# Gate products in column pairs, half of the inner dimension as seven-product blocks, and the first input split on VectorE

## The chip, the core and the metric

The kernel runs on one core of one Trainium2 chip. The metric is the device time of one launch in microseconds (us). Before the change three runs took 2828.03 to 2828.67 us, median 2828.26 us.

## What is computed

Two layers of a post-norm encoder for 256 tokens of width 2048, all in float32. A layer reads its input x (256 x 2048) and computes, cut to what matters:

```
h  = x @ w_in                      # 2048 x 4608: queries, keys, values of three mixers
ya, yb, yc = three attentions      # 1024, 512 and 512 wide
ga, gb, gc = split(sigmoid(x @ w_gate + b_gate), 3)          # 2048 x 6144
mix = ga * (ya @ w_br_a) + gb * (yb @ w_br_b) + gc * (yc @ w_br_c)
x  = layer_norm(ALPHA * x + mix @ w_out)
g, u = split(x @ w_ffn_in, 2)                                # 2048 x 11264
x  = layer_norm(ALPHA * x + (silu(g) * u) @ w_ffn_out)       # 5632 x 2048
```

## The kernel before

**Float32 by three products.** Every operand is held as a high part in the matmul's own number type and a low part that is the rest. A product is three matmuls: high by high, high by low, low by high. `split_unit` (L69) makes the parts of a weight block of 256 x 512 (two k-steps of 128): ACT casts the high part (`wh`), DVE subtracts it (`wl`). There are 5 buffers for raw blocks (`raw`) and 6 for each of `wh` and `wl`, so the splits run at most 6 blocks ahead of TensorE. SP's queue issues the loads in order. The parts of x (`xh`, `xl`) are the stationary operands, 128 x 128, for the two token tiles t = 0, 1.

**The plain product.** `gemm` (L94) computes 512 columns: for each block two k-steps, two token tiles and three matmuls, 12 matmuls on 512 columns. Its accumulators are two of the four banks of `psA`. After each block `pump` lets one step of side work (`side`: head transposes, attention) into the program.

**Two columns together.** In the feed-forward part `pair_gemm` (L571) computes the gate column and the up column of one 512-wide chunk f together, in seven accumulator banks p1, p6, p7, p2, p3, q4, q5. Of the 16 k-steps, 0 to 3 go as a seven-product block (Strassen's scheme in Winograd's form, over two halves of k and the two token tiles), 4 and 5 as a smaller one of single k-steps, and the others (`four`, L606) as plain products that add into the same banks. In all 61 steps of three matmuls, 183 matmuls, where two plain columns take 192. The sums that the scheme needs: of x by `x_sums` (L530, once a layer, as side work), of the weight blocks on DVE inside `pair_gemm` (`u`, `hub`, `e`, L620 to L647). Eight operations at its end (L660 to L667) join the banks. The block `hub` lives in two buffers of its own, not in `raw`. Chunk f = 0 goes by two plain products, under which `x_sums` runs; chunks 1 to 10 go by `pair_gemm`.

**Feed-forward groups.** Chunks 0 to 2, 3 to 5, 6 to 8 and 9 to 10 form four groups. After each chunk two token tiles are multiplied out (L684 to L691), transposed on TensorE (`hidTp`, L692) and split (`rl`, L694). After each group four columns of w_ffn_out are multiplied (L700) and added to the residual.

**Gates.** Twelve plain columns of w_gate, four per branch (L425 to L449). Each is followed by its column of the branch's projection, of 4 or 2 blocks. After the very first one the remaining side work is drained (L435).

**Start.** `x_lhs` (L152) loads the two tiles of a 512-wide chunk of x, transposes them on TensorE, casts on ACT and subtracts on DVE.

**End.** The last column of the last group takes its last 8 k-steps token tile by token tile (`tail=8`, L701), so that the layer norm of tile 0 can begin under the matmuls of tile 1.

The order on each engine is made by the scheduler of the kernel's language from data dependences and the program's order; each engine then works through its list in order. The page numbers the lines of the whole file; the functions that the change touches:

Of the kernel before, what the change touches and what calls it, by code (L numbers as in the profile page):

```python
# [33 lines left out]
def trunk_kernel(ctx: ExitStack, tc: tile.TileContext, x, w_in, sinks, lq1, lk1, lq2, lk2, diff_g,  # L34
# [33 lines left out]

    def split_unit(raw):  # L69
        h = wpool.tile([P, UK, CW], F32R, tag="wh", name="wh", bufs=6)  # L70
        l = wpool.tile([P, UK, CW], F32R, tag="wl", name="wl", bufs=6)
        n = raw.shape[1]
# [21 lines left out]
    def gemm(src, kw0, nk, c0, lhs, tail=0):  # L94
# [5 lines left out]
        def mm3(t, kt, w, j):  # L100
            (wh, wl), (ah, al) = w, lhs(kt, t)
            nc.tensor.matmul(acc[t], ah, wh[:, j, :], start=kt == 0, stop=False)  # L102
            nc.tensor.matmul(acc[t], ah, wl[:, j, :], start=False, stop=False)  # L103
            nc.tensor.matmul(acc[t], al, wh[:, j, :], start=False, stop=kt == nk - 1)  # L104

        for k in range(0, nk - tail, UK):
            lhs(k, 0)
            w = load_unit(src, kw0 + k, c0)
            for j in range(UK):
                for t in range(NT):  # L110
                    mm3(t, k + j, w, j)
# [13 lines left out]

    def bcast(vec, c0, name):
        t = scr.tile([P, CW], F32, tag="bc", name=name, bufs=4)
        nc.gpsimd.dma_start(t, vec[c0:c0 + CW].partition_broadcast(P))
        return t
# [16 lines left out]
    def set_x(c, t, src):  # L146
# [3 lines left out]
        split(xh[c][t], xl[c][t], pv)  # L150

    def x_lhs(kt, t):  # L152
        c = kt // 4
        if xh[c][t] is None:
# [3 lines left out]
            for u in range(NT):  # L158
                set_x(c, u, x0[u])
# [15 lines left out]
    for layer in range(DEPTH):  # L175
# [48 lines left out]
        def v_heads(acc, col0, slots):  # L224
            for i, s in enumerate(slots):
                for t in range(NT):
                    nc.scalar.copy(s[:, t * P:(t + 1) * P], acc[t][:, col0 + i * P:col0 + (i + 1) * P])

# [122 lines left out]
        sink = const.tile([P, AQ], F32, tag="sink", name="sink")  # L351
        nc.sync.dma_start(sink, sinks[layer].partition_broadcast(P))
        nsink = const.tile([P, AQ], F32, tag="nsink", name="nsink")
        nc.vector.tensor_scalar_mul(nsink, sink, -1.0)

        lv = const.tile([P, 4, 64], F32, tag="lv", name="lv")
        for i, v in enumerate((lq1, lk1, lq2, lk2)):
            nc.sync.dma_start(lv[:, i, :], v[layer].partition_broadcast(P))
        lp = const.tile([P, 2, 64], F32, tag="lp", name="lp")
        nc.vector.tensor_mul(lp, lv[:, 0::2, :], lv[:, 1::2, :])  # L360
        ls = const.tile([P, 2], F32, tag="ls", name="ls")
        nc.vector.tensor_reduce(ls, lp, AX.X, ALU.add)
        le = const.tile([P, 2], F32, tag="le", name="le")
        nc.scalar.activation(le, ls, AF.Exp)
        lam = const.tile([P, 1], F32, tag="lam", name="lam")
        nc.vector.tensor_sub(lam, le[:, 0:1], le[:, 1:2])
        nc.vector.tensor_scalar_add(lam, lam, lam_init)

        gcol = const.tile([P, 1], F32, tag="gcol", name="gcol")
        nc.sync.dma_start(gcol, diff_g[layer].rearrange("(p o) -> p o", o=1))  # L370
        nc.vector.tensor_scalar_mul(gcol, gcol, 1.0 - lam_init)
# [3 lines left out]
        relb = const.tile([P, NHC, 3 * P], F32, tag="relb", name="relb")  # L375
        for h in range(NHC):
            raw = tmp("hank")[:, :SEQ]
            row = rel_bias[layer, h]
            nc.sync.dma_start(raw, bass.AP(row.tensor, row.offset + 129, [[1, P], [1, SEQ]]))
            nc.vector.tensor_add(relb[:, h, 0:P], raw[:, 0:P][:, ::-1], mask_b[:, 0:P])  # L380
            nc.vector.tensor_add(relb[:, h, P:3 * P], raw[:, ::-1], mask_b[:, P:3 * P])
# [37 lines left out]
        mixT = [None] * NCH  # L419
        for b, (wbr, nk, y0i) in enumerate(((w_br_a, 8, 0), (w_br_b, 4, 2), (w_br_c, 4, 3))):  # L420
# [4 lines left out]
            for c in range(NCH):  # L425
                bg = bcast(b_gate[layer], b * D + c * CW, "bg")
                acc = gemm(w_gate[layer], 0, 16, b * D + c * CW, x_lhs)
                gs = []
                for t in range(NT):
                    g = tmp("gate")  # L430
                    nc.vector.tensor_add(g, acc[t], bg)
                    nc.scalar.activation(g, g, AF.Sigmoid)
                    gs.append(g)
                if b == 0 and c == 0:
                    drain()  # L435
                acc = gemm(wbr[layer], 0, nk, c * CW, y_lhs)
                for t in range(NT):
                    if b == 0:
                        mix[c][t] = act.tile([P, CW], F32, tag=f"fb{c * NT + t}", name=f"mix{c}{t}")
                        nc.vector.tensor_mul(mix[c][t], gs[t], acc[t])  # L440
                    else:
                        nc.vector.tensor_mul(gs[t], gs[t], acc[t])
                        nc.vector.tensor_add(mix[c][t], mix[c][t], gs[t])
                if b == 2:
                    mixT[c] = ychunk(c)
                    for t in range(NT):
                        pv = transpose4(mix[c][t], "mixTp")
                        s = slice(t * P, (t + 1) * P)
                        split(mixT[c][0][:, :, s], mixT[c][1][:, :, s], pv)  # L449
# [66 lines left out]


        sums = {}
        turn = [0]

        def sum_tiles():
            pair = const.tile([P, 2, 4, P], F32R, tag="relb", name="sums")
            for i in range(6):
                yield act.tile([P, 4, P], F32R, tag=f"fa{i}", name="sums")
            for i in range(2):
                yield pair[:, i]
            while True:
                yield scr.tile([P, 4, P], F32R, tag="bc", name="sums", bufs=4)

        def x_sums(delay):  # L530


            yield from wait(delay)
            tiles = sum_tiles()
            for c in range(NCH):
                z = []
                for t in range(NT):
                    v = tmp("z").rearrange("p (k q) -> p k q", k=4)
                    nc.vector.tensor_add(v, xh[c][t].bitcast(F32), xl[c][t].bitcast(F32))
                    z.append(v)  # L540
                yield
                n = (2, 1, 0, 0)[c]
                if n:
                    a11, a12, a21, a22 = (v[:, j:j + n, :] for v in z for j in (0, n))
                    p = tmp("zs").rearrange("p (k q) -> p k q", k=4)
                    q = tmp("zs").rearrange("p (k q) -> p k q", k=4) if n == 2 else p[:, 2:4]
                    s1, s2, s3, s4 = p[:, 0:n], p[:, n:2 * n], q[:, 0:n], q[:, n:2 * n]
                    nc.vector.tensor_sub(s1, a21, a22)
                    nc.vector.tensor_sub(s3, a11, a21)
# [204 lines left out]
```

## Time and profile before

| | us |
|---|---|
| runs, median (lowest to highest) | 2828.26 (2828.03 to 2828.67) |
| the profiled execution, its own time | 2827.89 |
| its span, first to last instruction | 2826.0 |
| busy: TensorE matmul (PE) | 2791.0 |
| busy: VectorE (DVE) | 1966.3 |
| busy: ScalarE (ACT) | 1349.6 |

The span is what the trace resolves; about 1.9 us of the execution lie around it. PE is busy for 99% of the span, in every slice but the first and the last; matmuls overlap in the pipeline, so a matmul's own duration (390 ns) is longer than the distance from one to the next. That distance, with the number of matmuls, is what sets the time.

### The profile page before, as it was taken

To read this page: it belongs to the slowest core of one execution; us is meant where nothing else is said; L and a number is where in the kernel's file an instruction comes from. 1 tells how busy PE (TensorE), PEld (TensorE's weight loads), DVE (VectorE), ACT (ScalarE), POOL (GpSimd) and SP (SyncE) were. 2 spreads that over 40 slices of the span, in tenths; PEclk is the share of its full clock that TensorE was granted. 3 is DMA by queue.
4 is the path that set the end of the run, shared out by engine and by line. 5 is a ranking of instruction groups with operands and counts; after the bars stand their busy time and mean duration, and the time that the engine had idled before them with its cause. 6 is when DMAs were issued, how large, how long until landed. Compare 5 with 4: busy or idle time off the path is not lost. (4 is left out here: it accounts for less than half of the span.)

```text
span 2826.0 us, 33866 instructions
## 1 busy us (share of the span) xinstructions
PE 2791.0 (99%) x12660; PEld 2296.8 (81%) x12660; DVE 1966.3 (70%) x2282; ACT 1349.6 (48%) x1722; POOL 60.7 (2%) x110
## 2 busy tenths in 40 slices
PE   8999999999999999999999999999999999999998
PEld 6887888887888888888878888888878888888886
DVE  5656555566986877868776565555579779688686
ACT  4455444443554544545445454444435545455452
POOL 0000000000000000000000000000000000000000
PEclk9999999999999999999999999999999999999999
DMA  7555666665665666665764556666656656656564
GB/s 255 171 164 175 202 200 205 203 209 177 198 204 190 194 202 193 194 201 177 229 216 153 179 177 202 201 204 202 209 162 214 200 190 196 203 186 208 186 198 141
DMA packets 282660, 549.20 MB, mean 194 GB/s; under 512 B 19840, under 2 KB 21376, under 8 KB 282496
## 3 DMA queue, kind: packets, MB, share of 16 engines
q1 hardware_dynamic: 276096, 526.07, 58.1%
q0 software_dynamic: 6400, 20.98, 2.6%
q8 instruction: 99, 1.62, 0.2%
q14 instruction: 65, 0.53, 0.1%
HBM read 542.78 MB, written 4.19 MB: 194 GB/s over the span
## 5 line engine op out<-in xcount | busy, mean ns | idle before, releaser
L74 DVE TENSOR_TENSOR wl<-raw,wh 128x1024 fp32r<-128x1024 f32 x972 | 1182.6, 1223 | 718.0 <-ACT wh L73 713.6
L73 ACT CAST wh<-raw 128x1024 fp32r<-128x1024 f32 x972 | 1019.2, 1054 | 1239.1 <-PE acc L104 809.4
L102 PE MATMUL acc<-wh,xh 128*128 128x512 f32 x1472 | 582.2, 396 | 6.9 <-ACT xh L54 6.9
L103 PE MATMUL acc<-wl,xh 128*128 128x512 f32 x1472 | 575.8, 391 | 3.6 <-DVE wl L74 2.0
L104 PE MATMUL acc<-wh,xl 128*128 128x512 f32 x1472 | 576.2, 392 | 0.2 <-DVE xl L55 0.2
L103 PE MATMUL acc<-wl,rh 128*128 128x512 f32 x1216 | 474.3, 390 | 0.0
L102 PE MATMUL acc<-wh,rh 128*128 128x512 f32 x1216 | 473.8, 390 | 0.0
L104 PE MATMUL acc<-wh,rl 128*128 128x512 f32 x1216 | 473.7, 390 | 0.0
L102 PEld LDWEIGHTS acc<-wh,xh 128*128 128x128 f32 x1472 | 277.1, 188 | 66.2 <-ACT xh L54 9.1
L103 PEld LDWEIGHTS acc<-wl,xh 128*128 128x128 f32 x1472 | 277.3, 188 | 61.9 <-DVE wl L74 4.1
L104 PEld LDWEIGHTS acc<-wh,xl 128*128 128x128 f32 x1472 | 277.0, 188 | 59.6 <-DVE xl L55 2.2
L102 PEld LDWEIGHTS acc<-wh,rh 128*128 128x128 f32 x1216 | 228.3, 188 | 47.3
L103 PEld LDWEIGHTS acc<-wl,rh 128*128 128x128 f32 x1216 | 228.3, 188 | 47.2
L104 PEld LDWEIGHTS acc<-wh,rl 128*128 128x128 f32 x1216 | 228.3, 188 | 46.9
L595 PE MATMUL q<-wh,xl 128*128 128x512 f32 x460 | 179.2, 390 | 0.0
L591 PE MATMUL q<-wh,xh 128*128 128x512 f32 x460 | 179.1, 389 | 0.0
L593 PE MATMUL q<-wl,xh 128*128 128x512 f32 x460 | 179.0, 389 | 0.0
L595 PE MATMUL p<-wh,sums 128*128 128x512 f32 x380 | 149.0, 392 | 0.0
L591 PE MATMUL p<-wh,sums 128*128 128x512 f32 x380 | 148.9, 392 | 0.0
L593 PE MATMUL p<-wl,sums 128*128 128x512 f32 x380 | 147.8, 389 | 0.0
L74 DVE TENSOR_TENSOR wl<-u,wh 128x1024 fp32r<-128x1024 f32 (+1 forms) x100 | 111.4, 1114 | 37.2 <-ACT wh L73 37.2
L73 ACT CAST wh<-u 128x1024 fp32r<-128x1024 f32 (+1 forms) x100 | 96.7, 967 | 78.6 <-PE p L595 39.8
(184 smaller groups left out, 2509.1 us busy)
## 6 DMA issues: line engine op xcount, KB each, us to landing
raw<-in_w_ffn_in_dram SPq DMA_DIRECT2D x332, 512.0 KB, 3.6
raw<-in_w_gate_dram SPq DMA_DIRECT2D x192, 512.0 KB, 4.2
raw<-in_w_ffn_out_dram SPq DMA_DIRECT2D x176, 512.0 KB, 3.7
raw<-in_w_in_dram SPq DMA_DIRECT2D x144, 512.0 KB, 3.6
raw<-in_w_out_dram SPq DMA_DIRECT2D x64, 512.0 KB, 4.0
raw<-in_w_br_a_dram SPq DMA_DIRECT2D x32, 512.0 KB, 4.1
hub<-in_w_ffn_in_dram SPq DMA_DIRECT2D x20, 512.0 KB, 3.4
raw<-in_w_br_b_dram SPq DMA_DIRECT2D x16, 512.0 KB, 4.6
```

What stands on the lines that cost most here:

```text
L73: nc.scalar.copy(h[:, 0:n], raw)
L74: nc.vector.tensor_sub(l[:, 0:n], raw, h[:, 0:n].bitcast(F32))
L102: nc.tensor.matmul(acc[t], ah, wh[:, j, :], start=kt == 0, stop=False)
L103: nc.tensor.matmul(acc[t], ah, wl[:, j, :], start=False, stop=False)
L104: nc.tensor.matmul(acc[t], al, wh[:, j, :], start=False, stop=kt == nk - 1)
L591: nc.tensor.matmul(bank[k], ah, wh[:, j, :], start=k not in begun, stop=False)
L593: nc.tensor.matmul(bank[k], ah, wl[:, j, :], start=False, stop=False)
L595: nc.tensor.matmul(bank[k], al, wh[:, j, :], start=False, stop=todo[k] == 0)
```

## The change

1. **Gates in pairs.** Ten of the twelve gate columns of a layer go as five calls of `pair_gemm` on neighbouring columns; the first two stay plain, and `x_sums` for the gates is drained after the second of them. The bias is loaded by `load_bias` into one buffer of `raw` in the middle of the pair, and added to p1 and q5 when the banks are joined. The two branch columns of a pair follow it.
2. **Half of k by the scheme.** `pair_gemm` is rewritten: k-steps 0 to 3 and 8 to 11 go as two seven-product blocks (`seven`), the other eight as plain `four`s that stand between. The steps are todo = 4 + 12 + 12 + 4 + 4 + 12 + 12 = 60, so 180 matmuls. `hub` is now a block of `raw` (w12). `x_sums` makes sums for all four chunks of x, once for the gates and once for the feed-forward part.
3. **Feed-forward groups** are chunks 0 to 3, 4 to 7 and 8 to 10: three instead of four.
4. **The first split of x** is made by DVE alone, cast and subtraction, in an order that is set: the second token tile's cast and subtraction are tied in front of the subtractions of the next two weight blocks. The loads and sums of the small constants of layer 0 and 1 are tied behind the last weight split of the first column.
5. **End:** `tail` is 12 in the last layer.

```diff
-        nc.scalar.copy(h[:, 0:n], raw)
-        nc.vector.tensor_sub(l[:, 0:n], raw, h[:, 0:n].bitcast(F32))
+        nc.scalar.copy(h, raw)
+        with tc.issue_after(behind.pop(0)) if behind else nullcontext():
+            split_ins.append(nc.vector.tensor_sub(l, raw, h.bitcast(F32)).ins)
...
-        split(xh[c][t], xl[c][t], pv)
+        if first is not None:
+            first.append(nc.vector.tensor_copy(xh[c][t], pv).ins)
+            first.append(nc.vector.tensor_sub(xl[c][t], pv, xh[c][t].bitcast(F32)).ins)
+        else:
+            split(xh[c][t], xl[c][t], pv)
...
-            for u in range(NT):
-                set_x(c, u, x0[u])
+            ins = []
+            with tc.issue_after(done[-2]) if done else nullcontext():
+                for u in range(NT):
+                    set_x(c, u, x0[u], ins)
+            behind[:] = [ins[2], ins[3]]
...
+            def seven(c, fill):
+                k1, k2 = 4 * c, 4 * c + 2
+                a11, a12, a22 = (part(xh[c][t], xl[c][t], j) for t, j in ((0, 0), (0, 2), (1, 2)))
+                s1, s2, s3, s4 = [part(h, l, j) for h, l in sums[c] for j in (0, 2)]
+                w12 = load_raw(src, k1, n2)
+                w22 = load_raw(src, k2, n2)
+                u = scr.tile([P, UK, CW], F32, tag="att", name="u", bufs=2)
+                nc.vector.tensor_add(u, w12, w22)
+                four(*fill[0])
+                prod("p7", s3, split_unit(u))
+                prod("p3", s4, split_unit(w22))
+                w11 = load_raw(src, k1, n1)
+                nc.vector.tensor_add(w12, w12, w11)
+                nc.vector.tensor_add(u, u, w11)
+                four(*fill[1])
+                prod("p1", a11, split_unit(w11))
+                prod("q5", s1, split_unit(w12))
+                prod("p6", s2, split_unit(u))
+                w21 = load_raw(src, k2, n1)
+                nc.vector.tensor_add(u, u, w21)
+                four(*fill[2])
+                prod("p2", a12, split_unit(w21))
+                for f in fill[3:-1]:
+                    four(*f)
+                prod("q4", a22, split_unit(u))
+                four(*fill[-1])
+
+            seven(0, [(4, n2), (6, n2), (12, n2), (4, n1)])
+            if load_bias:
+                bias = load_bias()
+            seven(2, [(14, n2), (6, n1), (12, n1), (14, n1)])
...
+                if b == 0 and c0 == 0:
+                    bgs = load_bias()
+                    side.append(x_sums(sums, 0))
+                    gates = []
+                    for c, bg in zip(cols, bgs):
+                        acc = gemm(w_gate[layer], 0, 16, c, x_lhs)
...
                     drain()
...
+                else:
+                    gates = pair_gemm(w_gate[layer], *cols, sums, load_bias)
...
-        groups = [range(0, 3), range(3, 6), range(6, 9), range(9, NFC)]
+        groups = [range(0, 4), range(4, 8), range(8, NFC)]
...
-                           tail=8 if last and c == NCH - 1 else 0)
+                           tail=(8 if layer < DEPTH - 1 else 12) if last and c == NCH - 1 else 0)
```

The lists that follow are of DVE, on which nearly all of the change's additions stand.

**At the end of a feed-forward pair.** `p` and `y` (from p2 and q4) are the last two joins, `sig` the multiplying out of the chunk, `rl` the splits of the transposed tiles, `u`, `hub` sums of weight blocks of the next pair. Before:

```order
L666 TENSOR_TENSOR p_7707<-p_7397,p_7707 128x512
L667 TENSOR_TENSOR y<-q_7394,y 128x512
L638 TENSOR_TENSOR u<-raw 128x512
L74 TENSOR_TENSOR wl<-hub,wh 128x1024
L685 TENSOR_TENSOR sig<-sig,p_7707 128x512
L685 TENSOR_TENSOR sig<-sig,y 128x512
L691 TENSOR_TENSOR sig<-sig,v 128x512
L691 TENSOR_TENSOR sig<-sig,c_7710 128x512
L74 TENSOR_TENSOR wl<-raw,wh 128x1024
L55 TENSOR_TENSOR rl_7726<-hidTp,rh_7725 128x4x128 x2
```

And in the changed kernel:

```order
L365 TENSOR_TENSOR p_10415<-p_10104,p_10415 128x512
L366 TENSOR_TENSOR y<-q_10101,y 128x512
L333 TENSOR_TENSOR u<-u,raw 128x1024
L688 TENSOR_TENSOR sig<-sig,p_10415 128x512
L688 TENSOR_TENSOR sig<-sig,y 128x512
L694 TENSOR_TENSOR sig<-sig,v 128x512
L694 TENSOR_TENSOR sig<-sig,c_10418 128x512
L78 TENSOR_TENSOR wl<-raw,wh 128x1024
L55 TENSOR_TENSOR rl_10434<-hidTp,rh_10433 128x4x128 x2
L78 TENSOR_TENSOR wl<-raw,wh 128x1024 x2
```

The place keeps its shape; the added sums and splits stand around it, a full weight sum where a half one stood.

**Under the first branch column of the gates.** `att`, `nm`, `rc` are the last attention head pair, `z`, `zs`, `sums` the sums of x, `mix` the first multiplied gate. Before, the attention stood there alone between weight splits:

```order
L74 TENSOR_TENSOR wl<-raw,wh 128x1024 x2
L55 TENSOR_TENSOR rl_2048<-y,rh_2047 128x512
L241 SCALAR_TENSOR_TENSOR att<-s,relb 128x384 x2
L246 TENSOR_REDUCE nm<-att 128x2 x2
L260 RECIPROCAL rc<-sm 128x4
L278 TENSOR_TENSOR att<-att,rc 128x2x128
L278 TENSOR_TENSOR att<-att,rc 128x2x256
L74 TENSOR_TENSOR wl<-raw,wh 128x1024 x2
L55 TENSOR_TENSOR rl_2048<-y,rh_2047 128x512
```

Now the sums of x stand behind it, between the splits of the pair's first blocks (with buffer numbers; `wl_2749` is the first block of the pair, `wl_2765` the second):

```order
L78 TENSOR_TENSOR wl_2749<-raw_2746,wh_2748 128x1024
L255 TENSOR_TENSOR z_2541<-xh11_173,xl11_174 128x512
L55 TENSOR_TENSOR sums_2532<-zs_2524,sums_2531 128x512
L55 TENSOR_TENSOR sums_2536<-zs_2525,sums_2535 128x512
L55 TENSOR_TENSOR rl3_2048<-y_2511,rh3_2047 128x512
L259 TENSOR_TENSOR z_2539<-z_2539,z_2541 128x512
L255 TENSOR_TENSOR z_2548<-xh20_222,xl20_223 128x512
L255 TENSOR_TENSOR z_2550<-xh21_231,xl21_232 128x512
...
L269 TENSOR_TENSOR zs_2553<-z_2548,zs_2552 128x256
L78 TENSOR_TENSOR wl_2765<-u_2744,wh_2764 128x1024
L55 TENSOR_TENSOR sums_2530<-zs_2552,sums_2530 128x512
```

Between the split of the last branch block and that of the pair's fourth block (`wl_2791`) stand 20 operations on 512 columns, 12 on 128 to 384, two maxima, one reciprocal and 6 of 1024 columns.

**At the start.** Before, the weight splits ran ahead of the second chunk of x:

```order
L74 TENSOR_TENSOR wl<-raw,wh 128x1024 x2
L55 TENSOR_TENSOR xl_107<-xTp,xh_106 128x512
L74 TENSOR_TENSOR wl<-raw,wh 128x1024
L55 TENSOR_TENSOR xl_116<-xTp,xh_115 128x512
L74 TENSOR_TENSOR wl<-raw,wh 128x1024 x3
L55 TENSOR_TENSOR xl_165<-xTp,xh_164 128x512
```

Now each chunk of x comes before the next two weight splits:

```order
L151 CAST xh_106<-xTp 128x512
L152 TENSOR_TENSOR xl_107<-xTp,xh_106 128x512
L151 CAST xh_115<-xTp 128x512
L78 TENSOR_TENSOR wl<-raw,wh 128x1024
L152 TENSOR_TENSOR xl_116<-xTp,xh_115 128x512
L78 TENSOR_TENSOR wl<-raw,wh 128x1024
L151 CAST xh_164<-xTp 128x512
L151 CAST xh_173<-xTp 128x512
L152 TENSOR_TENSOR xl_165<-xTp,xh_164 128x512
L152 TENSOR_TENSOR xl_174<-xTp,xh_173 128x512
L78 TENSOR_TENSOR wl<-raw,wh 128x1024 x2
```

TensorE's list there: the 8 transposes of a chunk, 24 matmuls on it, the next chunk's transposes, and so on; before, the second and third chunk's 16 transposes stood together after the first 24 matmuls.

## Rows read from the trace of the kernel before

**Rows 1.** The page: span, busy time of the engines, and TensorE's granted clock by slice.
```profile
span 2826.0 us, 33866 instructions
PE 2791.0 (99%) x12660; PEld 2296.8 (81%) x12660; DVE 1966.3 (70%) x2282; ACT 1349.6 (48%) x1722; POOL 60.7 (2%) x110
PEclk9999999999999999999999999999999999999999
```
**Rows 2.** Stages: stretch, length, busy us (count) by engine, clock, DMA share, GB/s.
```profile
897.50:1024.70 127.20, 126.66 (x567) 104.54 (x566) 109.55 (x118) 69.97 (x74) 0.00 (x0) 1.00 0.63 202
1024.70:1091.20 66.50, 66.50 (x298) 54.80 (x297) 41.21 (x42) 27.49 (x28) 0.00 (x0) 1.00 0.56 183
```
**Rows 3.** PE in order of time: eight matmuls that follow each other, first and last.
```profile
2811.71 0.39 PE L103 MATMUL acc<-wl,rh 128*128 128x512 f32 x1
...
2813.30 0.39 PE L104 MATMUL acc<-wh,rl 128*128 128x512 f32 x1
```
**Rows 4.** DVE in order of time around the end of a feed-forward pair.
```profile
941.64 0.69 DVE L685 TENSOR_TENSOR sig<-sig,p 128x512 f32<-128x512 f32 x1
942.25 0.68 DVE L685 TENSOR_TENSOR sig<-sig,y 128x512 f32<-128x512 f32 x1
...
976.35 1.22 DVE L626 TENSOR_TENSOR u<-u,raw 128x1024 f32<-128x1024 f32 x1
977.49 1.22 DVE L74 TENSOR_TENSOR wl<-raw,wh 128x1024 fp32r<-128x1024 f32 x1
980.13 1.23 DVE L74 TENSOR_TENSOR wl<-raw,wh 128x1024 fp32r<-128x1024 f32 x1 [1.43 <-ACT wh L73]
```
**Rows 5.** Waits: engine, line, whom it waited for; us in total, times, longest.
```profile
ACT wh L73 <- PE acc L104: 832.9, 515, 5.7
DVE wl L74 <- ACT wh L73: 750.8, 606, 7.4
PE hidTp L136 <- DVE sig L691: 3.2, 5, 1.1
```
**Rows 6.** The page: cast of a weight block on ACT; loads, us from issue to landing.
```profile
L73 ACT CAST wh<-raw 128x1024 fp32r<-128x1024 f32 x972 | 1019.2, 1054 | 1239.1 <-PE acc L104 809.4
...
raw<-in_w_ffn_in_dram SPq DMA_DIRECT2D x332, 512.0 KB, 3.6
raw<-in_w_gate_dram SPq DMA_DIRECT2D x192, 512.0 KB, 4.2
```
**Rows 7.** DVE in order of time, last attention head pair under the first branch column.
```profile
285.40 1.01 DVE L241 SCALAR_TENSOR_TENSOR att<-s,relb 128x384 f32<-128x384 f32 x2
286.44 1.01 DVE L246 TENSOR_REDUCE nm<-att 128x2 f32<-128x256 f32 x2
288.86 0.18 DVE L260 RECIPROCAL rc<-sm 128x4 f32<-128x4 f32 x1 [1.40 <-ACT att L252]
...
293.60 0.69 DVE L55 TENSOR_TENSOR rl<-y,rh 128x512 fp32r<-128x512 f32 x1 [1.23 <-ACT rh L54]
```
**Rows 8.** PE in order of time at the start.
```profile
4.36 1.94 PE L136 MATMUL xTp<-ident,x 128*128 128x128 f32 x8 [4.36 <-DMA x<-in_x_dram]
10.65 0.80 PE L102 MATMUL acc<-wh,xh 128*128 128x512 f32 x1 [4.35 <-ACT xh L54]
...
15.76 0.80 PE L102 MATMUL acc<-wh,xh 128*128 128x512 f32 x1 [2.51 <-ACT xh L54]
...
17.63 0.63 PE L102 MATMUL acc<-wh,xh 128*128 128x512 f32 x1
18.06 0.63 PE L103 MATMUL acc<-wl,xh 128*128 128x512 f32 x1
...
22.43 1.91 PE L136 MATMUL xTp<-ident,x 128*128 128x128 f32 x16
```
**Rows 9.** DVE in order of time at the end: tile 0's chain, then tile 1's first step.
```profile
2808.28 0.69 DVE L707 TENSOR_TENSOR r<-r,acc 128x512 f32<-128x512 f32 x1 [3.56 <-PE acc L104]
2815.41 0.68 DVE L707 TENSOR_TENSOR r<-r,acc 128x512 f32<-128x512 f32 x1
```

More of the change, by code (lines that the diff above doesn't have):

```diff
@@ L1 @@
 import math
[L2 removed]
+from contextlib import ExitStack, nullcontext
 import concourse.bass as bass
@@ L67, in load_raw @@
         return raw
+    behind = []
+    split_ins = []
+    done = []
     def split_unit(raw):
@@ L227, in v_heads, with sum_tiles, x_sums @@
                     nc.scalar.copy(s[:, t * P:(t + 1) * P], acc[t][:, col0 + i * P:col0 + (i + 1) * P])
+        def sum_tiles():
+            pair = const.tile([P, 2, 4, P], F32R, tag="relb", name="sums")
+            for i in range(6):
+                yield act.tile([P, 4, P], F32R, tag=f"fa{i}", name="sums")
+            for i in range(2):
+                yield pair[:, i]
+            for i in range(4):
+                yield scr.tile([P, 4, P], F32R, tag="bc", name="sums", bufs=4)
+        def x_sums(sums, delay):
+            yield from wait(delay)
+            tiles = sum_tiles()
+            for c in range(NCH):
+                z = []
+                for t in range(NT):
+                    v = tmp("z").rearrange("p (k q) -> p k q", k=4)
+                    nc.vector.tensor_add(v, xh[c][t].bitcast(F32), xl[c][t].bitcast(F32))
+                    z.append(v)
+                yield
+                if c % 2:
+                    nc.vector.tensor_sub(z[0], z[0], z[1])
+                    parts = [z[0]]
+                else:
+                    a11, a12, a21, a22 = (v[:, j:j + 2, :] for v in z for j in (0, 2))
+                    p, q = (tmp("zs").rearrange("p (k q) -> p k q", k=4) for _ in range(2))
+                    s1, s2, s3, s4 = p[:, 0:2], p[:, 2:4], q[:, 0:2], q[:, 2:4]
+                    nc.vector.tensor_sub(s1, a21, a22)
+                    nc.vector.tensor_sub(s3, a11, a21)
+                    nc.vector.tensor_sub(s2, a11, s1)
+                    yield
+                    nc.vector.tensor_sub(s4, a12, s2)
+                    parts = [p, q]
+                got = []
+                for v in parts:
+                    h, l = next(tiles), next(tiles)
+                    split(h, l, v)
+                    got.append((h, l))
+                    yield
+                sums[c] = got
@@ L514, in finish @@
                 nc.sync.dma_start(out[0, t * P:(t + 1) * P, c * CW:(c + 1) * CW], r[c][t])
+        groups = [range(0, 4), range(4, 8), range(8, NFC)]
+        stats = new_stats()
         sums = {}
[L519 to L528, printed above, removed]
@@ L680, in trunk_kernel @@
                     drain()
-                    accg, accu = pair_gemm(w_ffn_in[layer], f * CW, FFN + f * CW)
+                    accg, accu = pair_gemm(w_ffn_in[layer], f * CW, FFN + f * CW, sums)
                 for t in range(NT):
```

287 lines of the change are left out of this document (105 added, 182 removed).

## The prediction

> **What bounds the kernel now.** I read the page first, then a table of stages, then the engines' timelines at the places the change touches. The page is to show that TensorE has no room: 2791.0 of 2826.0 us busy, granted clock full in all slices, while DVE is busy for 70% [rows 1]. The sum is made against the profiled execution, 2827.89 us, its span of 2826.0 and 1.9 around it; that is 0.4 below the median of the runs. About 0.2%, 5.7 us, is what a measurement of this kernel can tell from no change.
>
> What a matmul costs is its distance to the next, not its duration: from the first to the last of eight that follow each other 1.59 us pass, 0.227 each [rows 3]. A feed-forward group bears this out: 288 matmuls (65.3) and eight short transposes fill a stage of 66.5 us [rows 2]. So three feed-forward pairs, 549 matmuls or 124.5 us, take 127.2, and TensorE idles there for 0.5 us. The engine is never short, because DVE and ACT run ahead and wait for it: 832.9 us of ACT's waits end with a matmul that frees a weight buffer [rows 5].
>
> The stages tell what DVE has left. In the three pairs it is busy for 109.6 of 127.2 us, in the group's product for 41.2 of 66.5 [rows 2]. By starts, an operation on 1024 columns costs DVE 1.14 us and one on 512 costs 0.60 [rows 4]; I use these. A pair has 24 of the first and 18 of the second, 38.2 us, against 183 matmuls and eight transposes, 42.3. So 4 us per pair are free.
>
> **What the change removes.** Each of the 20 feed-forward pairs loses 3 matmuls, each of the 10 gate pairs 12 of 192: 60 + 120 = 180, times 0.227 = **-40.8 us**, all on the path, since the engine is fed. The accumulating matmuls that replace others have the same shape and the same distance.
>
> One group less in each layer saves no matmul, only a change of stage, at 0.4 us each (66.5 less 288 matmuls and 0.8 for the transposes): **-0.8**. The eight residual additions less are DVE work that nothing waits for.
>
> At the end tile 0's chain holds DVE until 2815.41, when tile 1's first step starts; tile 1's last matmul starts at 2813.30, and tile 0's first step came 0.42 after the start of its own last matmul, 2807.86 by the distance [rows 3, 9]. With 12 steps by tile, tile 0 ends 2.7 us earlier and tile 1 could start at 2813.7: **-1.7**. DVE has no other work then but splits that precede.
>
> **What it adds on DVE.** A pair now has 22 splits and 8 sums on 1024 columns and, in the feed-forward part, 13 operations on 512: 30 x 1.14 + 13 x 0.60 = 42.0 us. TensorE has 180 matmuls and eight transposes: 41.7. The free 4 us are gone; DVE is as loaded as TensorE, and whatever stalls DVE now shows.
>
> The list at the pair's end gives the place. After the last matmul DVE does `y`, one `u`, four `sig` and the split of the second plain block: 0.60 + 1.14 + 2.40 + 1.14 = 5.3 us. TensorE meanwhile has the plain block (2.7), p7 (1.4), the transposes (0.8), which need the fourth `sig` at 4.1, and one more product (1.4) before it needs that split at 6.3. The transposes are due at 4.1 too: no room for the semaphores between. Waits of this kind exist already, 3.2 us in 5 cases [rows 5]. So 0.3 by the sum and 0.3 there, at the 14 pairs that follow a pair: **+8**. Ends: 0, if the lead carries it; 2 us each, 28, if ACT's sigmoids or a load come late as well.
>
> In the gates a pair with its two short branch columns costs DVE 34.2 + 10 x 0.60 + 8 x 0.60 (`mix`) + 4 x 1.14 = 49.6 us against 228 matmuls, 51.7: room of 2. But the bias holds one of the five `raw` buffers for the second half of the pair, and w12 another nearly always. With three left, a load is asked for only about three splits (3.4 us) before it is used, and a gate block takes 4.2 to land and 1.05 to be cast [rows 6]. DVE then idles 2 to 3 us per pair, most of it in its room: 0.5 at the eight pairs of branches two and three, **+4** (0 to 12). The pair of the first branch is followed by four more blocks and has room.
>
> The sums of x for the gates are the larger price. Between the split of the last branch block and that of the pair's fourth block stand, with that split, 20 operations by 0.60, 7 by 1.14, 12 smaller ones by at most 0.51 (half of the `att` pair, [rows 7]; 4.6 in all, as most have half its columns), two maxima (1.0) and a reciprocal: 25.8 us. With the largest lead, six blocks, TensorE can go on for 72 matmuls and the pair's first three blocks, 24 more: 21.8. It then lacks 4.0 us, less by the attention's short matmuls, more by 2.7 for each block of lead that is missing, and the chain has its own wait for ACT (1.40, [rows 7]). I take 6 per layer, **+12** (4 to 20). Before, the attention stood there without the sums.
>
> The second sums of a layer stand under 192 plain matmuls (43.5 us), as before: nothing.
>
> **The start.** TensorE gets its first matmul at 10.65, because ACT had two weight casts ahead of the cast of x, and has done two blocks by 22.43 [rows 8]. With DVE casting, it can begin when the first weight cast is done, near 7.4, and end two blocks some 5 us earlier. But the set order puts two casts, two subtractions and a split, 4 x 0.60 + 1.14 = 3.5 us, between the transposes of each further chunk and the second matmul on it, where before the splits stood ahead; TensorE has about 1 us to do. Three chunks by 2.5 us use up the gain: **0** (-4 to +3).
>
> **Sum:** 2827.9 - 40.8 - 0.8 - 1.7 + 8 + 4 + 12 + 0 = 2808.6, so **2809 us**.
>
> **The rivals.** (a) *Nothing is given back*: DVE's lead carries every place. 2827.9 - 43.3 = 2784.6. For it: TensorE idles for 0.5 us in 127.2 although the scheme is at work there [rows 2]. Against it: no room on DVE in a feed-forward pair.
>
> (b) *The clock falls.* At the start TensorE waited 2.51 us, and matmuls that follow are 0.43 apart (17.63, 18.06), 512 columns at 1.2 GHz, not 2.4 [rows 8]. If ten matmuls after each of three stalls in the gates of a layer stood so far apart, 0.20 more each, that is 12 us: 2821. Against it: the granted clock reads full in every slice [rows 1]. The Trainium skill, "TensorE: Matmul & The Clock Gate", Part 1, says that the clock is halved by default and after idling, and is released by activity; by that the stalls at the sums would be dearer than their length. The rows at the start agree in the spacing, the granted clock beside them does not show it.
>
> (c) *DVE becomes the bound, through the loads*, slower. w12 takes a `raw` buffer where `hub` had its own. If DVE idles for a load in each of the 60 half pairs, nothing hides it, since DVE has no room: 1 us each (4.2 + 1.05 against 4 splits, 4.5, [rows 4, 6]) gives 2827.9 - 43.3 + 12 + 60 = 2857. It decides from 0.5 us per half pair. Against it: three of five buffers stay free in the feed-forward part, and its loads land in 3.6.
>
> That the matmuls are not removed is excluded: the list of TensorE has 180 fewer.
>
> **Chances.** The forecast, 2791 to 2822: 0.58. (a) 0.22, (b) 0.04, (c) 0.10, and 0.06 for prices near the gain. The range for 8 in 10 reaches down to 2787, into (a) with a few us given back, and up to 2832, through (b): all upper ends at once would give 2847. Faster by over 0.2%: 0.58 + 0.22 and half of (b), 0.82; within 0.2%: 0.06 and the other half, 0.08; slower: 0.10.
>
> **What would show it.** Right: 180 matmuls fewer at the same distance; DVE busy for over 95% of a run of feed-forward pairs, with TensorE idle there by some tenths per pair on `sig` or `wl`; 4 us or more of waits for `wl` in the first gate pair of a layer; the first column ending near 42 us; tile 1's first step within 0.5 us of its last matmul. Wrong: waits for `wl` released by a load in most half pairs, matmuls 0.43 apart after a stall, or no idle time of TensorE in the gates.

## The result, and the profile after

The changed kernel takes **2853.2 us** (median of four runs, 2848.6 to 2857.7) against 2828.5 for the kernel before on the same chip (2828.0 to 2830.7): a ratio of **1.0086**, interval 1.0068 to 1.0104. It is slower by 25 us where 2809 was forecast, and its own runs lie 9 us apart where those of before lie within 3.

The profiled execution is the fastest of the four (2848.57, span 2846.8). Its page, beside [rows 1]:

```profile
span 2846.8 us, 33868 instructions
...
PE 2769.0 (97%) x12480; PEld 2268.9 (80%) x12480; DVE 2239.5 (79%) x2540; ACT 1428.1 (50%) x1806; POOL 60.3 (2%) x110
...
PEclk9999999999999999999999999999999999999999
```

The 180 matmuls are gone (12660 to 12480), but TensorE now idles for 78 us instead of 35. To see where, the span is cut at the same places of the program: up to the end of the first branch stage, from there through the gates and `w_out`, and the feed-forward part, for each layer. Columns as in [rows 2]. Before:

```profile
4.36:319.10 314.74, 306.80 (x1468) 251.94 (x1469) 194.34 (x292) 160.45 (x320) 8.71 (x14) 1.00 0.61 194
319.10:695.10 376.00, 375.61 (x1676) 310.40 (x1675) 215.51 (x223) 160.18 (x167) 9.77 (x17) 1.00 0.63 200
695.10:1414.90 719.80, 715.85 (x3202) 588.77 (x3200) 571.85 (x632) 359.34 (x383) 8.76 (x15) 1.00 0.61 198
1414.90:1719.60 304.70, 302.64 (x1459) 247.84 (x1457) 194.34 (x283) 155.81 (x312) 13.11 (x21) 1.00 0.58 183
1719.60:2095.60 376.00, 375.61 (x1678) 310.44 (x1676) 215.53 (x223) 160.22 (x167) 9.55 (x17) 1.00 0.64 199
2095.60:2813.50 717.90, 714.34 (x3189) 587.37 (x3186) 565.71 (x620) 352.33 (x375) 6.19 (x10) 1.00 0.59 191
```

and after:

```profile
4.19:325.40 321.21, 311.69 (x1468) 254.68 (x1469) 203.97 (x310) 158.47 (x315) 4.99 (x6) 0.99 0.56 177
325.40:711.30 385.90, 368.06 (x1617) 299.39 (x1616) 313.95 (x331) 187.44 (x199) 14.90 (x27) 1.00 0.63 205
711.30:1430.50 719.20, 710.01 (x3171) 584.37 (x3170) 599.77 (x625) 371.79 (x393) 7.64 (x13) 1.00 0.61 198
1430.50:1733.90 303.40, 302.11 (x1459) 248.20 (x1458) 203.32 (x313) 157.01 (x317) 8.88 (x13) 1.00 0.55 172
1733.90:2118.40 384.50, 368.96 (x1616) 300.38 (x1615) 313.78 (x331) 187.69 (x199) 14.83 (x27) 0.99 0.63 205
2118.40:2836.20 717.80, 707.92 (x3159) 581.86 (x3157) 597.64 (x623) 364.39 (x385) 6.17 (x10) 1.00 0.59 192
```

Read by the lengths: the gates with `w_out` have 60 matmuls fewer (13.6 us) and are 9.9 and 8.5 us *longer*; the feed-forward parts have 30 fewer (6.8 us) and are 0.6 and 0.1 shorter; the first stage is 6.5 longer in layer 0, where the start lies in it, and 1.3 shorter in layer 1. From the last matmul to the end of the span it is some 2 less.

The waits of the whole span name the places (us, times, longest):

```profile
ACT wh L76 <- DMA raw<-in_w_gate_dram: 121.4, 39, 9.0
...
ACT wh L76 <- DMA raw<-in_w_ffn_in_dram: 104.1, 71, 6.0
...
PE acc L106 <- DVE c L363: 17.6, 9, 3.2
...
DVE bg L357 <- DMA bg<-in_b_gate_dram: 13.2, 8, 2.1
```

Line 363 is the join c22, the last reader of p7. Its bank is the second that the branch product behind a gate pair takes. TensorE in order of time behind the last pair of layer 0:

```profile
608.59 0.51 PE L106 MATMUL acc<-wh,rh 128*128 128x512 f32 x1 [3.17 <-DVE c L363]
...
609.97 0.63 PE L107 MATMUL acc<-wl,rh 128*128 128x512 f32 x1
610.40 0.63 PE L108 MATMUL acc<-wh,rl 128*128 128x512 f32 x1
```

and DVE there:

```profile
594.91 2.36 DVE L78 TENSOR_TENSOR wl<-raw,wh 128x1024 fp32r<-128x1024 f32 x2 [3.63 <-ACT wh L76]
...
604.25 1.22 DVE L78 TENSOR_TENSOR wl<-raw,wh 128x1024 fp32r<-128x1024 f32 x1
605.38 0.68 DVE L362 TENSOR_TENSOR v<-v,bg 128x512 f32<-128x512 f32 x1
606.71 1.23 DVE L78 TENSOR_TENSOR wl<-raw,wh 128x1024 fp32r<-128x1024 f32 x1 [0.64 <-ACT wh L76]
607.85 0.68 DVE L363 TENSOR_TENSOR c<-v,p 128x512 f32<-128x512 f32 x1
```

DVE is late here because it stood 3.63 us for a weight block, and the joins stand singly between the splits of the branch blocks, so each late split holds up the joins behind it. L362 is also where the bias gives its `raw` buffer back. After the wait the matmuls are 0.43 apart, twice the usual distance; the granted clock (last but two in each line) of that stretch and of the next:

```profile
608.50:612.60 4.10, 4.01 (x11) 3.18 (x12) 4.10 (x6) 3.35 (x6) 0.00 (x0) 0.58 0.79 232
612.60:617.00 4.40, 4.40 (x21) 3.60 (x20) 3.53 (x5) 1.90 (x2) 0.14 (x1) 1.00 0.91 325
```

### The profile page after: what moved, and what is told of

It is laid out like the page before. It is cut to its first block, busy times and chain, and to the rows that moved or that the text cites. A ratio compares the mean times of both kernels' runs of the same rounds, so it can differ in the third digit from the quotient of the medians.

```text
span 2846.8 us, 33868 instructions
## 1 busy us (share of the span) xinstructions
PE 2769.0 (97%) x12480; PEld 2268.9 (80%) x12480; DVE 2239.5 (79%) x2540; ACT 1428.1 (50%) x1806; POOL 60.3 (2%) x110
## 4 chain that ended last, share of the span: by engine, by line
PE 31%; DVE 11%; DMA 5%; issue 2%; ACT 1%; DVEq 0%; ACTq 0%; SPq 0%
PE acc L106 7%; PE acc L108 7%; PE acc L107 7%; DVE wl L78 6%; DMA raw<-in_w_gate_dram 2%; DMA raw<-in_w_ffn_in_dram 2%; PE p L302 2%; PE p L304 2%; PE p L300 2%; PE q L302 1%; PE q L304 1%; PE q L300 1%; ACT wh L76 1%; DVE u L333 1%; DVE raw L332 0%
## 5 line engine op out<-in xcount | busy, mean ns | idle before, releaser
L106 PE MATMUL acc<-wh,rh 128*128 128x512 f32 x1216 | 478.6, 394 | 18.8 <-DVE c L363 17.6
L106 PE MATMUL acc<-wh,xh 128*128 128x512 f32 x832 | 334.1, 403 | 4.4 <-ACT wh L76 2.9
L107 PE MATMUL acc<-wl,xh 128*128 128x512 f32 x832 | 328.7, 395 | 8.7 <-DVE wl L78 7.0
L108 PE MATMUL acc<-wh,xl 128*128 128x512 f32 x832 | 328.3, 395 | 0.0
L76 ACT CAST wh<-u 128x1024 fp32r<-128x1024 f32 x180 | 189.1, 1051 | 211.7 <-DVE u L339 116.7
L300 PE MATMUL p<-wh,sums 128*128 128x512 f32 x600 | 235.3, 392 | 4.7 <-ACT wh L76 4.7
L302 PE MATMUL p<-wl,sums 128*128 128x512 f32 x600 | 233.9, 390 | 0.0
L78 DVE TENSOR_TENSOR wl<-u,wh 128x1024 fp32r<-128x1024 f32 x180 | 219.5, 1219 | 18.0 <-ACT wh L76 17.6
L304 PE MATMUL p<-wh,sums 128*128 128x512 f32 x600 | 233.6, 389 | 0.0
L107 PEld LDWEIGHTS acc<-wl,xh 128*128 128x128 f32 x832 | 158.2, 190 | 44.0 <-DVE wl L78 10.9
L302 PE MATMUL p<-wl,xh 128*128 128x512 f32 x480 | 187.5, 391 | 2.6 <-DVE wl L78 2.6
L106 PEld LDWEIGHTS acc<-wh,xh 128*128 128x128 f32 x832 | 157.4, 189 | 39.7 <-ACT wh L76 4.0
```

The source lines that it names most:

```text
L76: nc.scalar.copy(h, raw)
L78: split_ins.append(nc.vector.tensor_sub(l, raw, h.bitcast(F32)).ins)
L108: return nc.tensor.matmul(acc[t], al, wh[:, j, :], start=False, stop=kt == nk - 1)
L300: nc.tensor.matmul(bank[k], ah, wh[:, j, :], start=k not in begun, stop=False)
L302: nc.tensor.matmul(bank[k], ah, wl[:, j, :], start=False, stop=False)
L304: nc.tensor.matmul(bank[k], al, wh[:, j, :], start=False, stop=todo[k] == 0)
```

## The experiments

The twelve ran in three groups of four (e1 to e4, e5 to e8, e9 to e12), each on a chip of its own, on which the kernel before takes 2835.8, 2836.0 and 2836.8 us; each ratio is to runs of the kernel before that were taken beside it on the same chip. No trace of the kernel before was taken on these chips.

**e1: other banks for the branch product.**

```diff
-            for k in ("p3", "p7", "q5", "q4"):
+            lead = ("p1", "p6", "q5", "q4") if load_bias else ("p3", "p7", "q5", "q4")
+            for k in lead:
                 bank[k] = psA.tile([P, CW], F32, tag="acc", name=k)
-            for k in ("p1", "p6", "p2"):
+            for k in ("p3", "p7", "p2") if load_bias else ("p1", "p6", "p2"):
```

> The changed kernel, but in the gate pairs p1 and p6 take the first two banks of the pool that the next branch product allocates from, and p3 and p7 go to the other pool. Theory A (the branch product waits for p7's bank, which the join c22 gives back as one of the last of nine): in the changed kernel TensorE waits 17.6 us in 9 times for that join, and some matmuls behind the longest waits are at half clock, so 18 to 24 us go: 2825 to 2831 us, no wait for c22 left. Rival (VectorE is late as a whole, because the joins stand between the splits of the branch blocks): the same time comes back as waits for the splits wl, 2842 to 2849 us.

2854.78 us, ratio 1.0066 (1.0051 to 1.0081). TensorE's waits for c22 are gone, and the time is not: between 325 and 612 us TensorE now stands 4.3 us for `mix`, 5.4 for `wl` and 3.9 for `wh`. The bank is where the lateness shows, not where it comes from. The rival held in time; the waits came back for `mix` and `wh` as well as for `wl`.

**e2: the first x split as before.**

```diff
-            ins = []
-            with tc.issue_after(done[-2]) if done else nullcontext():
-                for u in range(NT):
-                    set_x(c, u, x0[u], ins)
-            behind[:] = [ins[2], ins[3]]
+            for u in range(NT):
+                set_x(c, u, x0[u])
```

> The changed kernel, but with the first x split as before (cast on ScalarE, no set order). Theory A (the set order ties each chunk's transposes and four operations of VectorE to the end of a block, 2 to 3 us idle three times, with matmuls at half clock behind): the first column ends near 41.5 instead of 48.6 us and the whole is 6 to 7 us shorter, 2842 us. Rival (what the start loses is taken back by the loads that run ahead meanwhile): under 2 us, 2847 us.

2839.64 us, ratio 1.0015 (1.0005 to 1.0024), 9 us below e3, its neighbour. The first operation on the first column's result starts at 38.79 instead of 48.76: more than the 6 to 7 expected, and better than before the change (42.18). The small constants still stand behind the first column, which may be why; no run separates it.

**e3: the norm parameters requested one column later.**

```diff
-        lnp = norm_params(ln1_g[layer], ln1_b[layer])
         for c in range(NCH):
+            if c == 1:
+                with tc.issue_after(done[-1]):
+                    lnp = norm_params(ln1_g[layer], ln1_b[layer])
```

The same for `ln2` in the last group.

> The changed kernel, but the parameters of both layer norms are loaded after the first column of the product that precedes the norm, not before it. Theory A (their 2 MB a time start when the sums of x give their buffers back, inside the last pair, and push that pair's weight loads from 4.4 to over 7 us): the stalls of 5 us in the last gate pair and of 3 to 5 us in the last feed-forward pair go in both layers, 14 to 18 us: 2831 to 2835 us. Rival (the held raw buffers alone make those loads late): the stalls stay, 2845 to 2850 us.

2848.61 us, ratio 1.0050 (1.0033 to 1.0067). This run decides nothing: the tie set a place in the program, not a wait, and GpSimd issued the first of these loads at 1322.57 against 1321.24. It serves below as the changed kernel on this chip: its trace spans 2846.5 us against 2846.8, with 120.4 us of waits for gate loads against 121.4. Its ratio is lower than the changed kernel's 1.0086 all the same, and why is not shown, so a price that is taken from e3 is uncertain by some 10 us.

**e4: the bias in two work tiles.**

```diff
                 def load_bias(cols=cols):
+                    ts = [tmp("bg") for _ in cols]
+                    for t, c in zip(ts, cols):
+                        nc.gpsimd.dma_start(t, b_gate[layer][c:c + CW].partition_broadcast(P))
+                    return ts
+
+                if b == 0 and c0 == 0:
                     t = wpool.tile([P, 2, CW], F32, tag="raw", name="bg", bufs=5)
                     for i, c in enumerate(cols):
                         nc.gpsimd.dma_start(t[:, i], b_gate[layer][c:c + CW].partition_broadcast(P))
-                    return t[:, 0], t[:, 1]
-
-                if b == 0 and c0 == 0:
-                    bgs = load_bias()
+                    bgs = t[:, 0], t[:, 1]
```

The first two, plain columns keep theirs in a `raw` buffer.

> The changed kernel, but a gate pair's bias is loaded into two of the small work tiles, so that all five raw buffers are for weights. Theory A (the bias' buffer is what makes the loads of a gate pair late): waits of the weight cast for a gate load fall from 121 us to under 60, TensorE's stalls inside gate pairs (2.8 in each layer's first, 5 in each last) go by half or more: 2838 to 2843 us. Rival (the loads are late for the norm parameters and for w12, the bias has nothing to do with it): within 3 us of the changed kernel, 2846 to 2851 us.

**2814.32 us** (2813.75 to 2814.89), ratio **0.9924** (0.9909 to 0.9939): 34 us below e3, several times what its own theory expected, and faster than before the change. The waits:

```profile
ACT wh L76 <- DMA raw<-in_w_gate_dram: 58.0, 25, 5.2
...
PE acc L106 <- DVE c L363: 2.8, 2, 1.8
```

The banks are as in the changed kernel, and c22 is nearly always in time. The gates with `w_out` in layer 0 fall from 385.9 us to 369.1 (in layer 1 from 384.5 to 368.6, so 32.7 of the 34 us lie here):

```profile
324.60:693.70 369.10, 364.38 (x1616) 300.10 (x1616) 312.88 (x331) 189.43 (x199) 14.95 (x27) 1.00 0.66 214
```

**e5: a raw buffer taken and given back at once.**

```diff
+                probe = scr.tile([P, 2, 1], F32, tag="probe", name="probe", bufs=2)
+                nc.vector.tensor_copy(probe, bias[2][:, :, 0:1])
...
+                    held = wpool.tile([P, 2, CW], F32, tag="raw", name="held", bufs=5)
```

> The bias in two small work tiles as in the run before, but a raw buffer is still taken at the same place, filled by the same two broadcasts, and given back where the bias was last used (a copy of two columns on VectorE, 8 bytes a partition, stands in for that use); nobody waits for the bias in the middle of the pair on its account. Theory A (what costs is the held buffer: three or four loads in flight instead of five): ratio to the kernel before 1.003 to 1.009, stalls of TensorE for c22 and in the last gate pairs as in the changed kernel. Rival (what costs is VectorE, standing in order at the sum of the two biases until their broadcast lands, 13 us in 8 waits): ratio 0.992 to 0.997.

2822.77 us, ratio 0.9956 (0.9941 to 0.9971), between the two. But the stand-in read was done by VectorE as soon as the buffer had landed (345.15 us in the first pair, which ends at 368.6), so the buffer was held, from the request of the broadcasts to that read, for 5 to 11 us in the first four pairs, not to the pair's end, and the run didn't test what was written.

**e9: the same, held to the pair's end.** The read now needs v:

```diff
+                probe = scr.tile([P, 1], F32, tag="probe", name="probe", bufs=2)
+                nc.vector.tensor_add(probe, v[:, 0:1], bias[2][:, 1, 0:1])
...
+                    held = wpool.tile([P, 2, CW], F32, tag="raw", name="held", bufs=5)
```

> As the run e5 with the held raw buffer, whose copy VectorE could do at once there, so that the buffer came free some 20 us before the pair's end; here the read needs the sum of v and the bias, the place where the changed kernel gave the buffer back. Theory A (the held buffer costs it all): the ratio of the changed kernel, 1.003 to 1.009, and TensorE waits for c22 behind the gate pairs again. Rival (that VectorE stands for the bias' broadcast costs most of it): 0.993 to 0.997, as e5, since nobody waits for this buffer's broadcast.

2858.83 us, ratio **1.0082** (1.0067 to 1.0097): the changed kernel's. Its waits, and the same stretch as above:

```profile
ACT wh L76 <- DMA raw<-in_w_gate_dram: 122.2, 42, 10.0
...
PE acc L106 <- DVE c L365: 19.1, 8, 3.1
...
DVE bg L357 <- DMA bg<-in_b_gate_dram: 2.0, 2, 1.1
```
```profile
324.40:714.40 390.00, 373.51 (x1617) 304.80 (x1616) 315.22 (x336) 188.52 (x199) 20.34 (x37) 0.97 0.64 209
```

(L365 is c22 there.) VectorE hardly waits for the bias (2.0 us against 13.2), and the losses are those of the changed kernel. Over the same four pairs the buffer is now held for 37 to 40 us each (35 to 40 in the changed kernel). The two more broadcasts of a pair, which the changed kernel doesn't have, are in e5 too, where everything that they and the short hold cost is 0.0032 of the ratio. So the buffer held for 0, for 5 to 11 and for 37 to 40 us gives 0.9924, 0.9956 and 1.0082.

**e6: e4 and e2 together.**

> The bias in two small work tiles and the first x split as before the change. Theory A (the two losses are independent: the first column ends 9 to 10 us earlier, the gates lose nothing for a held buffer): the sum of both, ratio 0.9885 to 0.990, first column near 38 us, 2803 us where the kernel before takes 2836. Rival (the lead that the start gives up is made good by later waits): ratio 0.991 or more.

2806.82 us (2806.22 to 2807.20), ratio 0.9899 (0.9885 to 0.9914). Within the intervals the two add up: the start gives 7.5 us here and 9 from e3 to e2.

**e10 and e11: which half of the new start costs.** Both with the bias in work tiles. e10 casts on VectorE in no set order (its diff is to e6), e11 on ScalarE in the set order (its diff is to e4).

```diff
             for u in range(NT):
-                set_x(c, u, x0[u])
+                set_x(c, u, x0[u], [])
```
```diff
-            first.append(nc.vector.tensor_copy(xh[c][t], pv).ins)
+            first.append(nc.scalar.copy(xh[c][t], pv).ins)
```

> The bias in two small work tiles, and the first x cast on VectorE as in the change, but in no set order. Theory A (the set order, which ties a chunk's transposes and casts behind a block and the weight splits behind them, costs the start): first column near 38 us as with the old start, ratio 0.989 to 0.990. Rival (the cast on VectorE itself, four operations a chunk in series where two engines shared them): first column 45 us or later, ratio 0.991 to 0.993.

> The bias in two small work tiles, and the first x cast on ScalarE as before, but in the set order of the change. The other half of the run beside it: by theory A (the set order) first column 45 us or later, ratio 0.991 to 0.993; by the rival (the cast on VectorE) near 38 to 40 us, 0.989 to 0.990.

e10: 2804.26 us, ratio 0.9890 (0.9874 to 0.9907). e11: 2813.23 us, ratio 0.9920 (0.9906 to 0.9935), as e4. VectorE's first operation on the first column's result, in the changed kernel and in e10 (in e11 it starts at 40.27):

```profile
48.76 0.42 DVE L199 TENSOR_TENSOR rope<-acc,ca 128x256 f32<-128x256 f32 x1 [1.19 <-PE acc L108]
```
```profile
37.70 0.42 DVE L196 TENSOR_TENSOR rope<-acc,ca 128x256 f32<-128x256 f32 x1
```

e11's first column is early, against its expectation, but its second is late: the second result is taken up at 66.37, in e6 at 60.17. By the end of the second column the set order costs 6 us with the cast on ScalarE (e11 against e6) and 11 on VectorE (70.09 in e4 against 59.28 in e10); the cast on VectorE by itself costs nothing.

**e7: e6 with the norm parameters truly late,** asked for behind the second column, with a wait:

```diff
+                nc.gpsimd.tensor_copy(t[:, 0:1], late[:, 0:1])
                 nc.gpsimd.dma_start(t, v[c * CW:(c + 1) * CW].partition_broadcast(P))
```

> The run beside it, and the norm parameters' loads now depend on the second column of the product ahead of the norm (GpSimd first copies one column of that result into the parameter's tile), so they can't run during the last pair. Theory A (their broadcasts, six within 8 us, take the DMA engines from the weights of the last feed-forward pair, where one load landed after 7.5 us): TensorE's gap of 3.4 to 4.9 us there goes in both layers, 6 to 10 us less than the run beside it. Rival (the gap comes from SyncE, which had no raw buffer to load into for 7.8 us): the gap stays within 1 us, and the time within 3 us of the run beside it.

**2791.47 us** (2789.77 to 2794.10), ratio **0.9846** (0.9830 to 0.9863), 15 us below e6 and the fastest version. In e6 TensorE stands in layer 1's last feed-forward pair, while six such broadcasts and the weights share the DMA engines (TensorE in order of time; the loads of the 25 us around, KB each and median us to landing; the stage):

```profile
2701.27 0.79 PE L299 MATMUL q<-wl,xh 128*128 128x512 f32 x1 [4.65 <-DVE wl L78]
```
```profile
raw<-in_w_ffn_in_dram SPq DMA_DIRECT2D x7, 512.0 KB, 7.3
```
```profile
2595.50:2727.70 132.20, 127.10 (x557) 104.19 (x556) 118.88 (x120) 73.72 (x77) 4.31 (x8) 0.97 0.65 205
```

The same stage of e7, where its loads land in 4.2:

```profile
2588.00:2713.00 125.00, 124.64 (x558) 102.82 (x557) 118.30 (x120) 73.35 (x77) 0.00 (x0) 1.00 0.64 199
```
```profile
raw<-in_w_ffn_in_dram SPq DMA_DIRECT2D x8, 512.0 KB, 4.2
```

Theory A holds. It gives 3.8 us in layer 0 and 7.2 in layer 1, in the stage of the last group's pairs, and some 2 in each layer from the last gate pair to the end of `w_out`: 15, more than the 6 to 10 expected.

**e8: the gates as before, all else as changed.**

```diff
-            for c0 in range(0, NCH, 2):
...
-                    gates = pair_gemm(w_gate[layer], *cols, sums, load_bias)
+            for c in range(NCH):
...
+                acc = gemm(w_gate[layer], 0, 16, b * D + c * CW, x_lhs)
```

> The changed kernel with the gates' part as before the change (plain columns, the bias in its own buffer, no sums of x there); the start, the feed-forward part and the tail as changed. Theory A (the feed-forward part gains under 1 us a layer, the tail 2, the start loses 7): ratio 1.000 to 1.003, 2829 to 2837 us by the clock of the first chip. Rival (the feed-forward part loses what the change loses, by its loads): 1.006 or more.

2837.08 us, ratio 1.0006 (0.9996 to 1.0015). Theory A holds: without the gates' part the change gains nothing. What the feed-forward part, the tail and the start each do is not separated by this run.

**e12: seven raw buffers, five for each half, on e7.**

```diff
-        raw = wpool.tile([P, UK, CW], F32, tag="raw", name="raw", bufs=5)
+        raw = wpool.tile([P, UK, CW], F32, tag="raw", name="raw", bufs=7)
-        h = wpool.tile([P, UK, CW], F32R, tag="wh", name="wh", bufs=6)
-        l = wpool.tile([P, UK, CW], F32R, tag="wl", name="wl", bufs=6)
+        h = wpool.tile([P, UK, CW], F32R, tag="wh", name="wh", bufs=5)
+        l = wpool.tile([P, UK, CW], F32R, tag="wl", name="wl", bufs=5)
```

> The fastest version so far (bias in work tiles, old start, norm parameters late) with seven raw buffers and five each for the two halves, in the same memory. Theory A (what is left of the stalls are loads asked for too late): 3 to 8 us less, ratio 0.982 to 0.9835. Rival (the lead of the splits is what hides VectorE's bursts, and a block less of it costs at the sums and at the pairs' ends): 3 to 10 us more, 0.9855 to 0.988.

2795.33 us (2794.23 to 2796.49), ratio 0.9858 (0.9844 to 0.9873), 3.9 us more than e7 and at the near end of the rival. With the buffer free and the broadcasts moved, more buffers for loads at the price of one block of lead gain nothing.

## Why the prediction was wrong

One chain of runs, beside which the kernel before takes the same time, carries the account: e3, the changed kernel in effect, 2848.6; the raw buffer freed (e4), 2814.3; the set order taken out (e6), 2806.8; the norm parameters moved (e7), 2791.5. From first to last that is 57 us, and the last stands 44 below the kernel before. That this 44 is near the sum's pure gain, 40.8 + 0.8 + 1.7 = 43.3, is chance: e7 still pays for the sums of x and in the feed-forward pairs, its first column is earlier than that of the kernel before (38.8 and 42.2), and by their spans, taken on different chips, its trace is shorter by 36 (2789.9 and 2826.0).

- **The step that failed is the bias and w12 in the raw buffers, "+4 (0 to 12)".** The bias' part alone measured 34 us (e3 to e4), or 45 by the ratios of e9 and e4; w12 stayed in `raw` in every run, and its part is not known. The cause was named rightly: a buffer held, loads late, DVE idle. What failed is "most of it in its room". From the first gate pair of layer 0 to the end of the fifth, in the changed kernel and then in e4, DVE does the same work (246 us):

```profile
325.60:604.60 279.00, 264.74 (x1157) 214.28 (x1156) 246.27 (x254) 141.38 (x150) 10.68 (x20) 1.00 0.63 205
```
```profile
324.60:588.40 263.80, 261.30 (x1158) 215.29 (x1158) 246.22 (x255) 144.52 (x152) 10.20 (x19) 1.00 0.67 218
```

  It idles for 32.7 us instead of 17.6, so 3.0 more per pair, about the 2 to 3 that were forecast; but the stretch is 15.2 us longer, so none of that went into DVE's room. A sum over a pair doesn't show where idle time falls. It falls towards the pair's end (3.63 us at 594.91), where nine joins stand between the splits: late splits make c22 late, p7's bank stays taken, and TensorE stands for it up to 3.2 us behind nine of the ten gate pairs, with matmuls at half clock behind the longest waits. The sum never asked what is due when DVE is late. e1 shows that with other banks the wait only moves, and e5 and e9, which differ in how long the buffer is held, that the hold is the cause.
- The Trainium skill, "Perfetto Trace Analysis", Optimization Strategy, says that the same gap coming again and again can mean that the memory for the next tile can't be had, through too few buffers. The gap behind the gate pairs is of that kind: 17.6 us of waits for c22 with the buffer held, 2.8 without.
- **The start, 0 (-4 to +3), also failed:** +6.6 at the first column. The gain was there: the second block ends, and the next transposes start, at 17.73 instead of 22.43 [rows 8], 4.7 us earlier where 5 was forecast. The three chunks behind it were sized too small. From there to the first column it takes 31.0 us, before the change 19.8, so they lose 11.3, 3.8 each and not 2.5. Before, then the changed kernel:

```profile
42.18 0.42 DVE L192 TENSOR_TENSOR rope<-acc,ca 128x256 f32<-128x256 f32 x1 [0.88 <-PE acc L104]
```
```profile
17.73 1.03 PE L136 MATMUL xTp<-ident,x 128*128 128x128 f32 x8
...
22.04 0.78 PE L107 MATMUL acc<-wl,xh 128*128 128x512 f32 x1 [1.83 <-DVE wl L78]
```
```profile
22.00:25.20 3.20, 3.16 (x8) 2.51 (x9) 1.12 (x1) 0.00 (x0) 0.00 (x0) 0.51 0.25 88
```

  In the three chunks TensorE waits 6.2 us, 5.0 of them for the weight splits behind the set order, and behind two of the three long waits the granted clock falls (0.51 here), which the sum left to rival (b). The cost is the set order's; the cast on VectorE makes it larger (11 us for 6) but costs nothing without it (e10, e11).
- **Missing from the sum: the norm parameters,** 15 us (e6 to e7). Their loads fell into the last feed-forward pair before the change too, at no cost: the last two pairs and their transposes took 84.0 us there, and TensorE was busy throughout. But before, seven broadcasts were issued over 18.5 us, and now six within 8, in a pair whose room on DVE the prediction had filled. It didn't ask what else ran there. Which of the two made them dear, no run separates.
- **Right:** 180 matmuls fewer, at the old distance where nothing waits. The tail: tile 1's first step starts at 2836.45, its last matmul at 2836.02, and the tail shrinks by about 2 (1.7 forecast).
- **The feed-forward pairs, +8, came out near in size, in part by another way.** DVE is busy for 161.05 of 167.80 us in the middle group, 96%, as forecast. In e7 the feed-forward parts take 715.1 and 713.2 us: 4.7 less than before each, where 30 matmuls and a group less are worth 7.2. So 5 in all are given back, by traces from different chips. TensorE's waits for `sig` there are 5.0 us against 3.2 [rows 5]; where the rest goes is not shown.
- **The sums of x, +12 (4 to 20), were too dear:** in e7 layer 1's first stage is 1.4 us shorter than before and in layer 0 the pair behind it takes 45.3 for 40.8, so about 3 a layer, 6 in all. They show as one wait of 2.4 us for the cast of `u`, which ACT does behind that of w12, which DVE had summed late; not as four of DVE's splits.
- **Rivals.** (b), the clock, was real and not separate: 69 matmuls stand 0.4 us or so from the next, 26 before; by an estimate from these counts 43 x 0.20 = 9 us on top of the waits. What spoke against it could not: a slice of the page is 71 us long, and it reads 9 (90% or more) in every slice after the change too. The rule of the Trainium skill, "TensorE: Matmul & The Clock Gate", Part 1, that the clock is halved after idling, agrees with the row of granted clock 0.58 behind the wait for c22, so such waits were dearer than their length. (c) had the right end by a wrong place: its sign came, for ACT's waits for feed-forward loads rose from 24.4 to 104.1 us; but they are 95.6 in e7 too, where the feed-forward pairs lose little, so those waits were not the price. It looked for the held buffer under w12, not under the bias.

## What to carry to other kernels

A tile lent from a rotating pool costs the lead of that pool from its request until its *last reader's turn* in an in-order queue; look where that turn falls, who is late then, and whose memory they hold. A stall is paid where the late engine's next product is needed, so ask of each bank and buffer who takes it next, and not only whether an engine's work fits into a stage. When a change uses up an engine's room, list what else runs in the same stage and cost nothing before: here parameter loads.

## What was not expected of the hardware

With six GpSimd broadcasts of 256 KB within 8 us a 512 KB weight load beside them takes 7.3 us to land, without them 4.2 (e6 and e7, medians of 25 us). A wait of 3.17 us behind a full-speed stretch is followed by 4.1 us at a mean granted clock of 0.58; a wait of 1.83 us at the start by 3.2 us at 0.51, with matmuls 0.43 apart. A wait of 2.37 us in the first gate pair is followed by matmuls 0.23 apart, one of 2.38 us at the same place in e7 by six distances of 0.43: so the length of the wait alone doesn't tell. And the kernel before differs by 0.26% from the first chip to those of the experiments (2828.5 and 2835.8), though 512 columns pass in 0.227 us on both; where the 7 us lie no trace shows. So times are compared here by ratios taken on one chip, and stage lengths across chips only with that doubt.
